# Spreading the gathering tokens' rows by three DRAM transfers in 4 KB runs, and turning 14 chunks of u early instead of 15

## The chip, the cores and the metric

The kernel runs on one core of a Trainium2 chip. Its time is the device time of one execution in microseconds (us). The engines are TensorE (PE in the profile, its weight loads PEld), VectorE (DVE), ScalarE (ACT), GpSimd (POOL) and SyncE (SP). Transfers are issued from the queues of SyncE, ScalarE and GpSimd, and run on 16 DMA engines that they share; the profile calls their packets q1 (SyncE's), q10 (ScalarE's) and q0 (GpSimd's).

## The reference

One decoder layer over 256 tokens of 1024 channels, in float32: a mixer (retention and block-sparse attention, merged by gates, with a residual), and then an expert layer, whose core is:

```python
def peer(h, w_q, sub_keys, u_tab, v_tab):       # h: 256 tokens x 1024
    q = (ht @ w_q).reshape(T, PEER_HEADS, 2, half)
    s = jnp.einsum('thcd,hcnd->thcn', q, sub_keys).astype(jnp.float32)
    s1, i1 = lax.top_k(s[:, :, 0], PEER_TOPK)
    s2, i2 = lax.top_k(s[:, :, 1], PEER_TOPK)
    ...
    top_s, pos = lax.top_k(cand_s, PEER_TOPK)
    experts = jnp.take_along_axis(cand_i, pos, axis=-1)
    gates = jax.nn.softmax(top_s, axis=-1).astype(h.dtype)
    ...
        u = u_tab[ec]
        a = jax.nn.gelu(jnp.einsum('td,thkd->thk', hc, u), approximate=False)
        return jnp.einsum('thk,thkd->td', gc * a, v_tab[ec])
```

There are 8 heads, 16 chosen experts each, and 16384 experts with a row of u and a row of v.

## The kernel before

The program has four stages. The mixer and the queries are a list of `pieces`: blocks of 256 x 512 of a weight matrix (512 KB), four to a unit of 512 output columns. A piece is loaded into one of six slots (`raw_ring`) by SyncE's queue (`load`, L191), split into a high part on ScalarE (L137, `rhi`) and a low part on VectorE (L138, `rlo`), and multiplied on TensorE in three products (L219 to L221, or L228 to L230). The main loops (L757 and L1001) go through the pieces in order: at step i they load piece i + 4 and beyond, split piece i + 3, multiply piece i, and then take one step (`pump`) of each of a few open tasks, generators that hold a unit's epilogue cut into parts. Each engine runs its instructions in the order in which they were written, so an instruction that waits holds up all that stands behind it on its engine; the DMA issues of ScalarE and GpSimd stand in their order too.

The query weights are the last 16 pieces (`peer_w_q`, four units). When a unit is complete, `queries` copies its result on ScalarE (L564), TensorE multiplies it with the sub-keys (L573), ScalarE scales the scores (L577), and VectorE chooses experts from them (`topk`). Two loads of sub-keys stand among the query pieces and hold two slots until TensorE has turned them (L788).

Then comes the u stage: all 16384 rows of u in 128 chunks of 128 rows. A chunk is loaded (L621), turned by eight TensorE transposes into `turn` (L666) with two evacuations on ScalarE (L667), and multiplied with the 144 dense tokens (L1137); meanwhile one-hot products build the dense gates (L1064). The other tokens gather only their chosen rows: 64 of them by one path, and 48 more (NX, three groups of 16, NXG x NXP) by a second. For the 48, the normed rows `h2x` are spread in DRAM so that each of the 8 heads has its own copy: `h2y`, shaped [3 groups, 8 heads, 16 tokens, 1024]. The u stage reads a group back as 128 rows in its first steps (`rows_x`, L1118, on ScalarE's queue). Last comes the v stage over 128 chunks of v.

The epilogue of the last mixer unit, `residual(1)`, does the spreading from GpSimd's queue, while the first query pieces are multiplied: h2x out to DRAM (L553), another row copy in SBUF (L554), then the spread (L556).

During the mixer, `early_turns` turns every eighth chunk of u ahead of time, NPRE of them, chunks 7, 15, 23 and so on: for each, four loads of 128 KB on ScalarE's queue (L677), two 32x32-block transposes on VectorE (L682) and a write of 512 KB to `turned` in DRAM (L679). In the u stage such a chunk is loaded from `turned` (L642), and TensorE skips its transposes. `early_turns` has two buffers in turn, named `eraw` and `h2` to read into, `eT` and `hTf` to write. The fifteenth, chunk 119, has its loads, transposes and write at steps 59 to 64 of the main loop, in the last units of the mixer.

Of the kernel before, what the change touches and what calls it, by code (L numbers as in the profile page):

```python
# [23 lines left out]
D = 1024  # L24
KC = D // P
H = 8
# [4 lines left out]
NXP = 16  # L31
NXG = 3
# [11 lines left out]
LAG_G = 2  # L44
SCRATCH = 88
TOPK = 16
NPRE = 15
STEP = 8
PRE0 = 20
WARM = 8  # L50
# [14 lines left out]
def layer_kernel(ctx, tc, x, mix_norm_g, w_in, ret_w_branch, moba_q_gain, moba_k_gain, moba_w_branch,  # L65
                 rel_bias, w_out, ffn_norm_g, peer_w_q, peer_sub_keys, peer_u, peer_v,
                 c_rope, c_decay, c_col, c_bucket, out, dbg=None):
    nc = tc.nc
# [18 lines left out]
    def side():  # L87
        return psum["side"].tile([P, 512], F32, name="side")
# [4 lines left out]
    def raw_tile(n=1):  # L93

        i = raw_count[0] % RAWS
        raw_count[0] += n
        assert i + n <= RAWS
        return raw_ring[:, i] if n == 1 else raw_ring[:, i:i + n]
# [36 lines left out]
    def split_to(hi, lo, src, engine=V):  # L135

        A.activation(hi, src, AF.Copy)  # L137
        engine.tensor_tensor(lo, src, hi.bitcast(F32), op=OP.subtract)  # L138
# [14 lines left out]
    h2x = dr.tile([NX, D], F32, name="h2x")  # L153
    h2y = dr.tile([NXG, H, NXP, D], F32, name="h2y")
# [5 lines left out]

    turned = dr.tile([NPRE, P, D], F32, name="turned")
    ident = cp.tile([P, P], F32, name="ident")
# [8 lines left out]
    def t4(shape, name, dt=F32):  # L171
        return wk.tile(shape, dt, name=name, tag="t4", bufs=3)

    def t2(shape, name):
        return wk.tile(shape, F32, name=name, tag="t2", bufs=4)
# [334 lines left out]
    def residual(j):  # L510
        def epi(o):

            xg = []
            for t in range(NT):
                c = slice(512 * j, 512 * (j + 1))
                V.tensor_tensor(xt[:, t, c], xt[:, t, c], o[t], op=OP.add)
            for t in range(NT):
                c = slice(512 * j, 512 * (j + 1))
                a = t2([P, 512], "xg")
                V.tensor_tensor(a, xt[:, t, c], grow2[:, c], op=OP.mult)  # L520
                sq = t2([P, 512], "sq2")
                A.activation(sq, xt[:, t, c], AF.Square, accum_out=ss2[:, j, t:t + 1])
                xg.append(a)
            yield
            yield
            for t in range(NT):
                p = side()
                for c in range(4):
                    T.transpose(p[:, c * P:(c + 1) * P], xg[t][:, c * P:(c + 1) * P], ident)
                split_to(qk_h[j][:, :, t * P:(t + 1) * P], qk_l[j][:, :, t * P:(t + 1) * P],  # L530
                         p.rearrange("p (c q) -> p c q", c=4))
            if j == 0:
                return
            nc.gpsimd.dma_start(x1d, xt)  # L534
            V.tensor_tensor(ss2[:, 0], ss2[:, 0], ss2[:, 1], op=OP.add)
            V.tensor_scalar(ss2[:, 0], ss2[:, 0], 1.0 / D, EPS, op0=OP.mult, op1=OP.add)
            G.tensor_tensor(r2, ss2[:, 0], minus_half[:, :NT], op=OP.pow)
            yield
            V.scalar_tensor_tensor(h2, xt[:, 0, :], r2[:, 0:1], grow2, op0=OP.mult, op1=OP.mult)
            hn = t4([P, D], "hn2")  # L540
            V.scalar_tensor_tensor(hn, xt[:, 1, :], r2[:, 1:2], grow2, op0=OP.mult, op1=OP.mult)
            yield
            for src, t0, n0, n in ((h2, NG, P, NA - P), (hn, 0, 0, P)):
                for q in range(2):
                    k = slice(4 * q, 4 * q + 4)
                    p = side()
                    for c in range(4):
                        T.transpose(p[:, c * P:(c + 1) * P], src.rearrange("p (i k) -> p k i", k=KC)[:, 4 * q + c], ident)
                    pv = p.rearrange("p (c q) -> p c q", c=4)[:, :, t0:t0 + n]
                    A.activation(hTf[:, k, n0:n0 + n], pv, AF.Copy)  # L550
                yield

            nc.gpsimd.dma_start(h2x, h2[P - NX:])  # L553
            nc.gpsimd.dma_start(h2[NG:], h2[:NG])  # L554
            yield
            nc.gpsimd.dma_start(h2y, h2x.rearrange("(n i) d -> n i d", n=NXG)[:, None].to_broadcast([NXG, H, NXP, D]))  # L556
            yield
        return epi

    def queries(q):  # L560
# [67 lines left out]
    def load_any(i):  # L628
# [9 lines left out]
        elif i < len(pieces) + NK:  # L638
            c = i - len(pieces)
            if c % STEP == STEP - 1 and c // STEP < NPRE:  # L640
                u_raw[c] = raw_tile()
# [14 lines left out]
    def transpose_u(c):  # L656

        if c < NK and c % STEP == STEP - 1 and c // STEP < NPRE:
            u_T[c] = u_raw.pop(c)
# [9 lines left out]
    def early_turns(i):  # L669

        m, step = divmod(i - PRE0, 3)
        if step == 0 and -1 <= m < NPRE - 1:

            c = STEP * (m + 1) + STEP - 1
            src = peer_u[0, c * P:(c + 1) * P, :].rearrange("(b a) (g d) -> g a b d", a=32, g=4)
            for g in range(4):
                nc.scalar.dma_start(early[0][(m + 1) % 2][32 * g:32 * g + 32].rearrange("a (b d) -> a b d", b=4), src[g])  # L677
        if step == 2 and 0 <= m < NPRE:
            nc.scalar.dma_start(turned[m], early[1][m % 2])  # L679
        if step < 2 and 0 <= m < NPRE:  # L680
            k = slice(4 * step, 4 * step + 4)
# [36 lines left out]
    for q in range(2):  # L718
        for t in range(NT):
            n = slice(t * P, (t + 1) * P)  # L720
            A.activation(hh[q][:, :, n], sides[2 * t + q], AF.Copy)
    for q in range(2):
        for t in range(NT):
            n = slice(t * P, (t + 1) * P)
# [397 lines left out]
    for c in range(NK):  # L1122
# [12 lines left out]
        for k in range(KC):  # L1135
            n = c % 2 * NA
# [142 lines left out]
```

## Time and profile before

| | us |
|---|---|
| median of three runs | 1034.11 |
| lowest and highest of them | 1033.67 to 1040.05 |
| the profiled execution, its own time | 1033.85 |
| its span, first to last instruction | 1031.8 |

The stages in that execution: mixer to about 256, queries to about 332, u stage to about 730, then the v stage. The page gives each engine's busy time, the span in 40 slices of 25.8 us, and the chain that ended last, followed back from the last instruction. In the rows of a timeline stand start, duration (of a merged group, from its first start to its last end), engine, line, operation, what is written and read, the shapes, and, in brackets, how long the engine had been idle and what ended it. Rows of a window hold its length and then each engine's busy time with the number of instructions; rows of a DMA queue hold packets, MB and the time that its packets took, as a share of 16 engines for the window's length. Two of the transfer rows of the page:

```profile
q0 software_dynamic: 27008, 96.82, 26.0%
...
raw_ring<-turned SPq DMA_DIRECT2D x15, 512.0 KB
```

### The profile page before, as it was taken

Reading aid. Unit: us, or ns where it says so; the run is one execution under the profiler, and the core shown is the slowest. Engines: PE = TensorE matmul, PEld = TensorE weight load, DVE = VectorE, ACT = ScalarE, POOL = GpSimd, SP = SyncE. Lnnn points to the kernel's source line nnn. Section 1 sums busy time; section 2 is a strip of 40 time slices with the busy share of each in tenths; the row PEclk is TensorE's granted clock in tenths of the full one; section 3 lists DMA queues with packets and bytes.
Section 4 is the critical chain, followed back from the end, with each engine's and each line's share of the span. In section 5 each row is a group of like instructions: output and inputs, shape, how many; then the busy total and the mean of one; then the engine's idle time right before and its main releaser. Section 6 shows DMA issues by size and latency. Waiting matters only on the chain.

```text
span 1031.8 us, 19502 instructions
## 1 busy us (share of the span) xinstructions
PE 1005.6 (97%) x7384; PEld 967.9 (94%) x7384; DVE 815.1 (79%) x1482; ACT 546.1 (53%) x991; POOL 307.0 (30%) x256
## 2 busy tenths in 40 slices
PE   8999999999949999999999999999999999999997
PEld 6887998997949999999999999999999999999997
DVE  6567667978548895699977999994788888888887
ACT  5545544534524434443346776679655555555553
POOL 2421000000102344444443443542433333333330
PEclk9999999999969999999999999999999999999999
DMA  9775787987735999899999787887799999999993
GB/s 332 194 201 169 235 247 212 301 269 225 239 123 162 383 372 352 330 367 373 376 384 344 280 284 255 285 320 244 270 345 345 352 336 345 348 343 345 341 347 108
DMA packets 103067, 301.43 MB, mean 292 GB/s; under 512 B 10740, under 2 KB 21005, under 8 KB 102822
## 3 DMA queue, kind: packets, MB, share of 16 engines
q1 hardware_dynamic: 64732, 186.07, 52.1%
q0 software_dynamic: 27008, 96.82, 26.0%
q10 hardware_dynamic: 11234, 17.31, 5.4%
q8 instruction: 58, 0.95, 0.4%
q14 instruction: 35, 0.29, 0.1%
HBM read 289.15 MB, written 12.00 MB: 292 GB/s over the span
## 4 chain that ended last, share of the span: by engine, by line
PE 89%; DMA 3%; DVE 3%; ACT 2%; issue 1%; ACTq 0%; POOL 0%; DVEq 0%; POOLq 0%
PE acc L1137 24%; PE acc L1170 19%; PE turn L666 10%; PE acc L1171 8%; PE gp L1064 4%; PE acc L228 3%; PE acc L229 3%; PE acc L230 3%; PE acc L219 3%; PE acc L220 3%; PE acc L221 3%; DMA raw_ring<-in_peer_w_q_dram 2%; PE side L573 1%; PE side L349 1%; PE side L374 1%
## 5 line engine op out<-in xcount | busy, mean ns | idle before, releaser
L924 POOL DMA_INDIRECT rows<-in_peer_u_dram,eg x112 | 140.0, 1250 | 130.0 <-DVE rows L935 50.4
L924 POOL DMA_INDIRECT rows<-in_peer_v_dram,eg x64 | 106.8, 1669 | 168.3 <-DVE vacc L998 167.4
L666 PE MATMUL turn<-ident,raw_ring 128*128 128x128 f32 x904 | 118.5, 274 | 0.8 <-ACT W L577 0.8
L666 PEld LDWEIGHTS turn<-ident,raw_ring 128*128 128x128 f32 x904 | 110.0, 191 | 1.0 <-ACT W L577 1.0
L935 DVE SCALAR_TENSOR_TENSOR rows<-rows,h 128x1024 f32<-128x1024 f32 x64 | 78.4, 1229 | 8.6 <-DMA rows<-in_peer_u_dram,eg 8.5
L998 DVE SCALAR_TENSOR_TENSOR vacc<-rows,av,vacc 128x1024 f32<-128x1024 f32 x63 | 80.6, 1279 | 0.0
L1108 ACT ACTIVATE cw<-W 128x384 fp32r<-128x384 f32 x64 | 33.7, 526 | 81.9 <-PE acc L1171 31.7
L1109 DVE TENSOR_TENSOR cw<-W,cw 128x384 fp32r<-128x384 f32 x64 | 36.3, 568 | 33.7 <-ACT cw L1108 33.7
L1079 ACT ACTIVATE W<-gp 128x512 f32<-128x512 f32 (+18 forms) x48 | 27.5, 577 | 41.4 <-DVE W L1077 35.0
L1030 ACT ACTIVATE oh_buf<-oh_buf,tT 128x128 f32<-128x128 f32 x128 | 40.9, 407 | 0.4 <-DVE oh_buf L1026 0.4
L1077 DVE TENSOR_TENSOR W<-gp,W 128x328 f32<-128x328 f32 (+17 forms) x36 | 36.5, 1015 | 5.3 <-PE gp L1064 5.0
L1094 POOL TENSOR_TENSOR W<-W,gl 128x288 f32<-128x288 f32 (+17 forms) x24 | 15.6, 651 | 83.9 <-ACT gl L1093 77.8
L935 DVE SCALAR_TENSOR_TENSOR rows<-rows,rlo__3191 128x1024 f32<-128x1024 f32 x16 | 19.4, 1217 | 21.1 <-DMA rows<-in_peer_u_dram,eg 21.0
L1064 PE MATMUL gp<-oh_buf 128*128 128x128 f32 x256 | 33.8, 276 | 0.0
L1137 PE MATMUL acc<-hTf,raw_ring 128*128 128x144 f32 x240 | 31.9, 286 | 0.0
L1064 PEld LDWEIGHTS gp<-oh_buf 128*128 128x128 f32 x256 | 31.5, 191 | 0.1
L1137 PEld LDWEIGHTS acc<-hTf,raw_ring 128*128 128x128 f32 x240 | 30.3, 190 | 0.0
L534 POOL DMA_DIRECT2D x1d<-xt x1 | 0.7, 652 | 91.7 <-DMA raw_ring<-in_peer_w_q_dram 91.7
L1025 DVE TENSOR_TENSOR oh_buf<-niota,tT 128x512 f32<-128x512 f32 x32 | 22.1, 690 | 7.0 <-PE gp L1064 6.4
L144 POOL TENSOR_TENSOR gny<-va,minus_half 128x8 f32<-128x8 f32 x2 | 3.3, 1653 | 79.1 <-DVE va L436 79.1
L935 DVE SCALAR_TENSOR_TENSOR rows<-rows,rlo__3252 128x1024 f32<-128x1024 f32 x16 | 19.3, 1218 | 9.4 <-DMA rows<-in_peer_u_dram,eg 9.4
L1026 DVE TENSOR_TENSOR oh_buf<-iota,tT 128x512 f32<-128x512 f32 x32 | 25.4, 793 | 0.0
(2091 smaller groups left out, 3491.2 us busy)
## 6 DMA issues: line engine op xcount, KB each, us to landing
raw_ring<-in_peer_v_dram SPq DMA_DIRECT2D x128, 512.0 KB
raw_ring<-in_peer_u_dram SPq DMA_DIRECT2D x113, 512.0 KB
raw_ring<-in_w_in_dram SPq DMA_DIRECT2D x52, 512.0 KB
raw_ring<-in_peer_w_q_dram SPq DMA_DIRECT2D x16, 512.0 KB
raw_ring<-turned SPq DMA_DIRECT2D x15, 512.0 KB
eraw<-in_peer_u_dram ACTq DMA_DIRECT2D x32, 128.0 KB
turned<-eT ACTq DMA_DIRECT2D x8, 512.0 KB
raw_ring<-in_ret_w_branch_dram SPq DMA_DIRECT2D x8, 512.0 KB
```

What stands on the lines that cost most here:

```text
L666: T.transpose(p[:, k * P:(k + 1) * P], r.rearrange("p (i k) -> p k i", k=KC)[:, 4 * q + k], ident)
L924: G.indirect_dma_start(out=r, out_offset=None, in_=tab, in_offset=bass.IndirectOffsetOnAxis(ap=eg[:, j:j + 1], axis=0))
L935: V.scalar_tensor_tensor(r, r, 1.0, h, op0=OP.mult, op1=OP.mult, accum_out=av[:, j:j + 1])
L998: V.scalar_tensor_tensor(gs["acc"], r, av[:, j:j + 1], gs["acc"], op0=OP.mult, op1=OP.add)
L1030: A.activation(o1[:, j], o1[:, j], AF.Copy, scale=tT[:, t, 2, k + j:k + j + 1])
L1064: T.matmul(p[:, j * P:(j + 1) * P], o2, o1, start=True, stop=True)
L1077: V.tensor_tensor(w[:, :, :c], p[:, :, :c], w[:, :, :c], op=OP.mult)
L1108: A.activation(w[:, :, :ND], W[:, c:c + 2, :], AF.Copy)
L1109: V.tensor_tensor(w[:, :, ND:], W[:, c:c + 2, :], w[:, :, :ND].bitcast(F32), op=OP.subtract)
L1137: T.matmul(pa[:, n:n + NA], uT[:, k * P:(k + 1) * P], hTf[:, k], start=(c % 2 == 0 and k == 0), stop=(k == KC - 1), skip_group_check=True)
L1170: T.matmul(o[b][:, :2 * ND], vh[:, n], w, start=(c == 0), stop=False, skip_group_check=True)
L1171: T.matmul(o[b][:, :ND], vl[:, n], w[:, :ND], start=False, stop=(c == NK - 1), skip_group_check=True)
```

## The change

```diff
-NPRE = 15
+NPRE = 14
...
             nc.gpsimd.dma_start(h2x, h2[P - NX:])
             nc.gpsimd.dma_start(h2[NG:], h2[:NG])
             yield
-            nc.gpsimd.dma_start(h2y, h2x.rearrange("(n i) d -> n i d", n=NXG)[:, None].to_broadcast([NXG, H, NXP, D]))
-            yield
+            for n in range(NXG):
+                src = h2x[NXP * n:NXP * (n + 1)]
+                nc.gpsimd.dma_start(h2y[n].rearrange("h i d -> i h d"), src[:, None, :].to_broadcast([NXP, H, D]))
+                yield
```

The spread of the 48 rows becomes three transfers, one for a group, with the 16 tokens outermost, the 8 copies inside them, and runs of one row (4 KB). Each is followed by a `yield`, so they go out in three steps of the task. And chunk 119 of u isn't turned early any more. Lines behind L556 move down by two in the changed kernel.

On GpSimd's queue, from the write of x1d to the first gathers of u; `h_74` is the tile of the normed rows. Before:

```order
L534 DMA x1d<-xt 128x2048
L537 TENSOR_TENSOR r_75<-ss_116,minus_half 128x2
L553 DMA h2x<-h_74 48x1024
L554 DMA h_74<-h_74 64x1024
L556 DMA h2y<-h2x 24x1x16384
L867 DMA eg<-ei 64x16
L924 DMA rows<-in_peer_u_dram,eg 128x1024 x5
```

After:

```order
L534 DMA x1d<-xt 128x2048
L537 TENSOR_TENSOR r_75<-ss_116,minus_half 128x2
L553 DMA h2x<-h_74 48x1024
L554 DMA h_74<-h_74 64x1024
L558 DMA h2y<-h2x 16x8x1024 x3
L869 DMA eg<-ei 64x16
L926 DMA rows<-in_peer_u_dram,eg 128x1024 x5
```

One transfer of 24 blocks of 16 rows became three of 16 x 8 single rows, in the same place.

On VectorE, near the end of the mixer, where chunk 119 was turned (`sa` and `ml` belong to the epilogue of a mixer unit, `rlo` are low parts of weights). Before:

```order
L138 TENSOR_TENSOR rlo__2196<-raw_ring,rhi__2195 128x1024
L682 STREAM_TRANSPOSE eT<-eraw 128x4x4x32
L138 TENSOR_TENSOR rlo__2226<-raw_ring,rhi__2225 128x1024
L504 TENSOR_TENSOR sa<-sa,acc 128x512
L505 TENSOR_TENSOR sa<-sa,sb 128x512
L138 TENSOR_TENSOR ml_139<-sa,mh_137 128x512
L504 TENSOR_TENSOR sa<-sa,acc 128x512
L505 TENSOR_TENSOR sa<-sa,sb 128x512
L138 TENSOR_TENSOR ml_139<-sa,mh_137 128x512
L682 STREAM_TRANSPOSE eT<-eraw 128x4x4x32
L138 TENSOR_TENSOR rlo__2264<-raw_ring,rhi__2263 128x1024
```

After (the numbers of the tiles shift a little):

```order
L138 TENSOR_TENSOR rlo__2192<-raw_ring,rhi__2191 128x1024
L138 TENSOR_TENSOR rlo__2221<-raw_ring,rhi__2220 128x1024
L504 TENSOR_TENSOR sa<-sa,acc 128x512
L505 TENSOR_TENSOR sa<-sa,sb 128x512
L138 TENSOR_TENSOR ml_139<-sa,mh_137 128x512
L504 TENSOR_TENSOR sa<-sa,acc 128x512
L505 TENSOR_TENSOR sa<-sa,sb 128x512
L138 TENSOR_TENSOR ml_139<-sa,mh_137 128x512
L138 TENSOR_TENSOR rlo__2258<-raw_ring,rhi__2257 128x1024
```

The two transposes are gone and nothing else moved; ScalarE's queue loses the four loads and the write.

On TensorE, in the u stage at chunk 119. Before:

```order
L1064 MATMUL gp<-oh_buf 128x128 x4
L1137 MATMUL acc<-hTf,rhi__6986 128x144 x8
L1064 MATMUL gp<-oh_more 128x128 x4
L666 MATMUL turn<-ident,raw_ring 128x128 x8
L1137 MATMUL acc<-hTf,rhi__7023 128x144 x8
L1064 MATMUL gp<-oh_buf 128x128 x4
L666 MATMUL turn<-ident,raw_ring 128x128 x8
L1137 MATMUL acc<-hTf,raw_ring 128x144 x8
```

After:

```order
L1066 MATMUL gp<-oh_buf 128x128 x4
L668 MATMUL turn<-ident,raw_ring 128x128 x8
L1139 MATMUL acc<-hTf,rhi__6981 128x144 x8
L1066 MATMUL gp<-oh_more 128x128 x4
L668 MATMUL turn<-ident,raw_ring 128x128 x8
L1139 MATMUL acc<-hTf,rhi__7018 128x144 x8
L1066 MATMUL gp<-oh_buf 128x128 x4
L668 MATMUL turn<-ident,raw_ring 128x128 x8
L1139 MATMUL acc<-hTf,rhi__7059 128x144 x8
```

Chunk 119 gets the eight transposes that every untouched chunk has (and two evacuations on ScalarE), and its products read the turned copy in place of the loaded rows.

## The prediction

> **What bounds the kernel now.** I read the page first: busy time per engine, the slices, the chain that ended last.
>
> ```profile
> span 1031.8 us, 19502 instructions
> PE 1005.6 (97%) x7384; PEld 967.9 (94%) x7384; DVE 815.1 (79%) x1482; ACT 546.1 (53%) x991; POOL 307.0 (30%) x256
> PEclk9999999999969999999999999999999999999999
> PE 89%; DMA 3%; DVE 3%; ACT 2%; issue 1%; ACTq 0%; POOL 0%; DVEq 0%; POOLq 0%
> ```
>
> TensorE bounds the program: busy for 97% of the span, and 89% of the chain. So an edit is worth what it puts on or takes off TensorE's time, and the only places with something to take off are those where TensorE stands. The twelfth slice of the clock, a 6 among nines, is one. The windows around it, and the chain of waits in order of time there, say what it is:
>
> ```profile
> 270.00:280.00 10.00, 10.00 (x88) 10.00 (x88) 3.33 (x5) 5.92 (x10) 0.37 (x1) 1.00 0.72 218
> 280.00:290.00 10.00, 5.62 (x47) 5.42 (x46) 2.17 (x16) 0.59 (x1) 0.00 (x0) 0.89 0.41 163
> 290.00:300.00 10.00, 1.32 (x6) 1.32 (x7) 3.16 (x15) 3.09 (x4) 0.00 (x0) 0.50 0.36 121
> 300.00:310.00 10.00, 10.00 (x68) 10.00 (x68) 8.49 (x37) 4.17 (x5) 0.00 (x0) 0.76 0.46 155
> ...
> 275.24 21.74 DMA raw_ring<-in_peer_w_q_dram
> ```
>
> In the windows the columns are TensorE, its weight loads, VectorE, ScalarE, GpSimd, then the granted clock, the DMA share and GB/s. TensorE is full until 285, nearly empty to 298, and then runs at a clock of 0.50, mean 0.76 in the ten us after. What ended last was a load of a query-weight piece that took 21.74 us, with DMA only 0.36 to 0.46 busy: it was blocked, not short of bandwidth. The timelines of GpSimd, SyncE's queue and ScalarE:
>
> ```profile
> 269.74 0.63 POOL L556 DMA_DIRECT2D h2y<-h2x  x1
> ...
> 271.50 0.37 SPq L191 DMA_DIRECT2D raw_ring<-in_peer_w_q_dram  x1
> 275.24 0.37 SPq L191 DMA_DIRECT2D raw_ring<-in_peer_w_q_dram  x1
> ...
> 279.90 0.69 ACT L577 ACTIVATE W<-side,r 128x512 f32<-128x512 f32 x1 [0.21 <-PE side L573]
> 295.75 1.06 ACT L137 ACTIVATE rhi__2735<-raw_ring 128x1024 fp32r<-128x1024 f32 x1 [15.16 <-DMA raw_ring<-in_peer_w_q_dram]
> ...
> 298.68 3.78 PE L573 MATMUL side<-skT,W 128*128 128x128 f32 x16 [13.06 <-ACT W L564]
> ```
>
> The load of 271.50 (of the piece that rhi__2735 splits) was issued just behind h2y, the transfer that the change rewrites. ScalarE stood 15.16 us for it, the copy L564 was queued behind, and TensorE stood 13.06 us for that copy. The DMA queues from 284.1 to 292, the middle of the stall (packets, MB, share of 16 engines):
>
> ```profile
> q0 software_dynamic: 9, 0.59, 17.5%
> ...
> q1 hardware_dynamic: 9, 0.02, 0.6%
> ```
>
> q0 (GpSimd's queue) moves nine packets of 0.59 MB / 9 = 65 KB, each 0.175 x 16 x 7.9 / 9 = 2.46 us, on 0.175 x 16 = 2.8 engines at a time: h2y, 24 packets for three engines, 8 x 2.46 = 20 us. q1 (the weights) gets nine of 2 KB in the same time: one behind each big one. Every weight piece is spread over all the engines and waits for its last packets on those three.
>
> **The change, part by part.** (1) The three transfers. Each spreads 16 rows, eight times over: 128 packets of 4 KB, 384 in all instead of 24, same 1.5 MB. GpSimd issues two more transfers at about 0.63 us each; between 270.4 and the next thing that it does it has nothing to do:
>
> ```profile
> 321.11 0.55 POOL L867 DMA_DIRECT2D eg<-ei  x1 [50.74 <-DVE i12f L876]
> ...
> 334.19 0.33 ACTq L1118 DMA_DIRECT2D rlo__3191<-h2y  x1
> ```
>
> so they cost nothing on the path, and the rows are read back only at 334. What a 4 KB packet from DRAM to DRAM takes, the trace doesn't show. From below: a sixteenth of the 65 KB packet, 0.154 us. From above: the 4 KB packets from SBUF to SBUF (L554), alone on the engines in the window 270.2 to 271.4:
>
> ```profile
> q0 software_dynamic: 59, 0.24, 90.8%
> ```
>
> 0.908 x 16 x 1.2 / 59 = 0.30 us, on 14.5 engines at once. I take 0.2, nearer to the lower end, because the old packets are the only ones that go from DRAM to DRAM. With 24 packets for each of 16 engines that is 4.8 us (3.7 to 7.2). A weight piece is 256 packets of 2 KB, 16 an engine, whose price is in the window 276 to 282:
>
> ```profile
> q1 hardware_dynamic: 793, 1.54, 76.4%
> ```
>
> 0.764 x 16 x 6 / 793 = 0.092 us, 1.5 us a piece. Worst case, all of h2y goes first: the loads of 271.50 and 275.24 are through 3.0 + (3.7 to 7.2) = 6.7 to 10.2 us after about 272.5 (the first issue, and a us that I allow for the start), at 279 to 283. These are times of before; part (2) moves all of them alike. The first is wanted when ScalarE is free at 280.6, and shares the engines with h2y packet by packet: 16 x (0.092 + 0.2) = 4.7 us, there at 277. The second has to be split (1.06 us) ahead of L564, which TensorE allows at 285.3, so it is wanted by 284.2. Both make it, at both ends of the bound. The stall then goes as a whole; how much that is, I read by laying the same place of the next unit, which has no stall, beside it:
>
> ```profile
> 285.34 0.28 PE L230 MATMUL acc<-hh,rlo__2640 128*128 128x256 f32 x1
> 302.12 0.56 PE L228 MATMUL acc<-hh,rhi__2682 128*128 128x256 f32 x1
> 304.81 0.29 PE L228 MATMUL acc<-hh,rhi__2682 128*128 128x256 f32 x1
> ...
> 314.77 0.28 PE L230 MATMUL acc<-hh,rlo__2831 128*128 128x256 f32 x1
> 317.15 0.36 PE L228 MATMUL acc<-hh,rhi__2877 128*128 128x256 f32 x1
> 318.66 0.28 PE L228 MATMUL acc<-hh,rhi__2877 128*128 128x256 f32 x1
> ```
>
> From the last product of a unit to the thirteenth of the next (L573's 16 small products lie between): 318.66 - 314.77 = 3.89 us without the stall, 304.81 - 285.34 = 19.47 with it, by when the clock is full again. The difference, 15.58 us, is the stall and its cold clock (13.06 and 2.52).
>
> Why three engines, and will it be sixteen? The trace shows both kinds: 2.8 engines for h2y, 14.5 for the 64 rows of L554. In the Trainium skill, "DMA: Bandwidth & Descriptors", section "Queues, rings and completion order", the number of engines is the largest up to 16 that divides the slowest dimension of both sides. That gives 3 for h2y now (3 groups against 24 blocks), which agrees with the 2.8 above, and 16 after the change (16 rows on both sides); without that rule the sum goes by the row of L554.
>
> (2) The fifteenth early chunk leaves the mixer: four loads that ScalarE's queue issues, two transposes on VectorE, a write of 512 KB. VectorE there, two rows of the chain of waits, ScalarE and TensorE:
>
> ```profile
> 231.08 1.22 DVE L682 STREAM_TRANSPOSE eT<-eraw 128x512 f32<-128x512 f32 x1
> 238.75 1.17 DVE L682 STREAM_TRANSPOSE eT<-eraw 128x512 f32<-128x512 f32 x1
> 239.84 1.18 DVE L138 TENSOR_TENSOR rlo__2264<-raw_ring,rhi__2263 128x1024 fp32r<-128x1024 f32 x1
> ...
> 232.30 1.11 DVE rlo__2226 L138
> ...
> 237.48 0.64 ACT mh L137
> ...
> 238.01 1.04 ACT L137 ACTIVATE rhi__2263<-raw_ring 128x1024 fp32r<-128x1024 f32 x1
> ...
> 241.08 0.50 PE L220 MATMUL acc<-rlo__2264,mh 128*128 128x512 f32 x1 [1.46 <-DVE rlo__2264 L138]
> ```
>
> TensorE stands 1.46 us for rlo__2264. The chain runs from the first transpose through VectorE and ScalarE to ScalarE's mh, right ahead of rhi__2263, so without that transpose all of this comes 1.2 us earlier. Without the second, rlo__2264 starts when rhi__2263 is there, at 239.05 - 1.2 = 237.85 instead of 239.84, and ends at 239.0, before TensorE asks for it at 239.6. All of the 1.46 us goes. With the second alone it would be 0.8 (239.05 for 239.84): my lower end. The freed issues and the write lie on queues that nobody waits for once this is gone.
>
> (3) The same chunk, 119, is turned by TensorE in the expert stage instead. The chain has the price, where any chunk stands:
>
> ```profile
> 336.95 0.89 PE turn L666 x8
> 337.84 1.96 PE acc L1137 x16
> ...
> 660.00:670.00 10.00, 10.00 (x87) 10.00 (x87) 10.00 (x13) 5.72 (x20) 6.07 (x6) 1.00 0.54 161
> ```
>
> +0.89 us of TensorE, all of it on the path, since TensorE has no gap in that stage. Two evacuations on ScalarE (2 x 0.54 us) fit: it is 5.72 of 10 us busy there. VectorE is full, but gets no more work, only 0.89 us more time. The load is the same 512 KB from another place.
>
> Sum: 1033.85 (this execution's own time; 2 us lie around its span) - 15.58 - 1.46 + 0.89 = 1017.7 us. Its own time is 0.26 us under the median of the runs shown, so I give it unchanged.
>
> **The rivals.** A shorter stall stays: 4 KB packets now stand on every engine, not on three. It begins when 3.0 + 24 x p passes 284.2 - 272.5 = 11.7 us, at p = 0.36 us a packet, above my bound of 0.30; at 0.5 us the stall is 3.3 us, and the time 1021. A gap of 1.46 us left the clock full:
>
> ```profile
> 240.00:250.00 10.00, 8.68 (x40) 6.85 (x41) 8.96 (x11) 7.16 (x11) 0.00 (x0) 1.00 0.77 255
> ```
>
> one of 13.06 did not, so up to 1.3 us of cold clock may be added, for 1022 to 1023. The Trainium skill ("TensorE: Matmul & The Clock Gate", Part 1) has the clock recover after about 3.4 us of sustained work. By it today's cold clock would be worth 1.7 us; the rows above have it last from 298.68 to 304.8 and cost 2.52, and they decide. Chance 0.13.
>
> The change doesn't do what it says: the transfers stay on few engines. Then 384 packets x 0.2 / 3 = 26 us, but each weight packet there waits for a 4 KB packet, not for one of 65 KB: 16 x 0.29 = 4.7 us a piece, 9.4 for the first two, there at 282. Even that stalls little: about 1018 to 1022, as the later pieces come every 4.7 us to a TensorE that wants one about every 3.3. 0.07.
>
> VectorE takes over, with the top-k work no longer hidden by the stall. From where the stall ends to where the last query piece is split:
>
> ```profile
> 296.84:320.33 23.49, 19.62 (x59) 0.83 0.45 147
> ```
>
> 19.62 us of VectorE's work for that. Begun at 281.7 it ends at 301.4 at the earliest; TensorE comes to that piece at about 310 (the eighth from 285.34 + 2.38 = 287.7: seven of 24 x 0.12 = 2.9 us, and 2.3 for the next L573). It has 8 us in hand; chance 0.03, time up to 1021.
>
> Slower than before: the same mechanism as the first rival, with a packet so dear that all sixteen engines block longer than three do. Stall and cold clock are back to today's when 3.0 + 24 x p reaches 11.7 + 13.06, at p = 0.91 us; 1% slower, 1044, needs about 1.4 us. Against it: three times the upper end of the bound. 0.03.
>
> **How the numbers follow.** My forecast, 1017.7, has 0.74; with the ends of its terms (0.8 for 1.46; L573's copy or a load late by a us or so) it is 1016.5 to 1020. The range takes in the shorter stall: 1016 to 1023. About 1% is what a measurement of this kernel can tell from no change, here 1023.8 and 1044.5. Faster: the forecast, VectorE, nearly all of the shorter stall and of the few engines, 0.91. Same: the rest of these, 0.06. Slower 0.03.
>
> **What would show it.** Right: no idle time of TensorE above 2 us between 230 and 320, PEclk 9 in all slices, the chain without DMA on the query weights; 384 q0 packets of 4 KB within some 8 us after the issue; TensorE without a gap at L220; one more group of eight transposes. Wrong: ScalarE waiting for a query piece around 280, which by its length gives the packet's price, or a new wait of TensorE for VectorE behind it.

## The result, and the profile after

| | before | changed |
|---|---|---|
| median of four runs | 1034.72 us | 1017.54 us |
| lowest and highest | 1033.67 to 1040.05 | 1016.8 to 1020.45 |
| the profiled execution, its own time | 1033.85 | 1016.8 |
| its span | 1031.8 | 1015.0 |

The ratio is 0.9839, with a 95% interval of 0.9814 to 0.9864: the kernel is 1.4 to 1.9% faster. The forecast was 1017.7 us.

The page of the changed kernel, busy time of each engine, the clock in 40 slices, and the shares of the chain that ended last:

```profile
span 1015.0 us, 19518 instructions
...
PE 1003.3 (99%) x7392; PEld 966.3 (95%) x7392; DVE 812.3 (80%) x1480; ACT 547.3 (54%) x993; POOL 303.2 (30%) x258
...
PEclk9999999999999999999999999999999999999999
...
PE 95%; ACT 2%; DVE 1%; DMA 1%; issue 1%; ACTq 0%; POOL 0%; SPq 0%; DVEq 0%; POOLq 0%
```

TensorE's busy time is about what it was (1003.3 us for 1005.6); the span around it is 16.8 us shorter. The 6 among the nines is gone, and the chain has 1% DMA left of 3%. The windows that were half empty before, columns as there:

```profile
270.00:280.00 10.00, 10.00 (x87) 10.00 (x87) 4.70 (x18) 5.47 (x8) 0.00 (x0) 1.00 0.99 321
280.00:290.00 10.00, 9.97 (x82) 9.57 (x81) 8.39 (x44) 5.82 (x8) 0.00 (x0) 1.00 0.72 252
290.00:300.00 10.00, 9.97 (x82) 9.57 (x81) 9.86 (x16) 4.10 (x6) 0.00 (x0) 1.00 0.52 165
...
230.00:320.00 90.00, 89.12 (x652) 83.69 (x652) 71.58 (x188) 44.65 (x67) 9.74 (x13) 1.00 0.70 224
```

TensorE works through all of them, at a granted clock of 1.00 (before: 5.62 and 1.32 us of ten, clock 0.89 and 0.50). From 230 to 320 it is idle for 0.88 us in all. What stands in the place of the 13 us stall, first ScalarE (the splits of two query pieces, then the copy L566, which was L564), then TensorE:

```profile
279.12 1.06 ACT L137 ACTIVATE rhi__2730<-raw_ring 128x1024 fp32r<-128x1024 f32 x1 [0.50 <-DMA raw_ring<-in_peer_w_q_dram]
280.69 1.06 ACT L137 ACTIVATE rhi__2769<-raw_ring 128x1024 fp32r<-128x1024 f32 x1 [0.51 <-DMA raw_ring<-in_peer_w_q_dram]
283.03 1.31 ACT L566 ACTIVATE W<-acc 128x512 f32<-128x512 f32 x2 [1.28 <-PE acc L230]
...
283.37 0.28 PE L230 MATMUL acc<-hh,rlo__2635 128*128 128x256 f32 x1
283.68 2.32 PE L575 MATMUL side<-skT,W 128*128 128x128 f32 x16
285.75 0.37 PE L228 MATMUL acc<-hh,rhi__2677 128*128 128x256 f32 x1
```

ScalarE still waits for both loads, by half a us each instead of 15.16 us for one. It then waits 1.28 us for TensorE at L566: the loads came 1.28 us before they would have held anyone up.

To see where the time went I compare when TensorE starts the same instruction in both kernels, which needs no reading of idle time:

| place | this step | after minus before, so far |
|---|---|---|
| start of the mixer's main part (differs from run to run) | +0.45 | +0.45 |
| the products around L220, near 240 | -1.79 | -1.34 |
| the products around L529, near 246, and little bits up to the queries | -0.63 | -1.97 |
| from the last product of the second query unit to the thirteenth of the third | -15.57 | -17.54 |
| chunk 119 in the u stage | +0.89 | -16.65 |
| end of the v stage | -0.04 | -16.69 |

The steps give 16.7 of the 16.8 us by which the spans differ.

### The profile page after: what moved, and what is told of

It is laid out like the page before. It is cut to its first block, busy times and chain, and to the rows that moved or that the text cites. A ratio compares the mean times of both kernels' runs of the same rounds, so it can differ in the third digit from the quotient of the medians.

```text
span 1015.0 us, 19518 instructions
## 1 busy us (share of the span) xinstructions
PE 1003.3 (99%) x7392; PEld 966.3 (95%) x7392; DVE 812.3 (80%) x1480; ACT 547.3 (54%) x993; POOL 303.2 (30%) x258
## 4 chain that ended last, share of the span: by engine, by line
PE 95%; ACT 2%; DVE 1%; DMA 1%; issue 1%; ACTq 0%; POOL 0%; SPq 0%; DVEq 0%; POOLq 0%
PE acc L1139 25%; PE acc L1172 19%; PE turn L668 10%; PE acc L1173 9%; PE acc L228 4%; PE acc L229 4%; PE acc L230 4%; PE gp L1066 4%; PE acc L219 4%; PE acc L220 3%; PE acc L221 3%; PE side L575 1%; PE side L349 1%; DMA raw_ring<-in_w_in_dram 1%; PE side L374 1%
## 5 line engine op out<-in xcount | busy, mean ns | idle before, releaser
L926 POOL DMA_INDIRECT rows<-in_peer_u_dram,eg x112 | 136.5, 1218 | 133.7 <-DVE rows L937 52.3
L1139 PE MATMUL acc<-hTf,raw_ring 128*128 128x144 f32 x224 | 29.8, 286 | 0.0
```

Source lines behind the costliest of these rows:

```text
L926: G.indirect_dma_start(out=r, out_offset=None, in_=tab, in_offset=bass.IndirectOffsetOnAxis(ap=eg[:, j:j + 1], axis=0))
L1139: T.matmul(pa[:, n:n + NA], uT[:, k * P:(k + 1) * P], hTf[:, k], start=(c % 2 == 0 and k == 0), stop=(k == KC - 1), skip_group_check=True)
```

## The experiments

My theory: the stall came from packets of 65 KB on three engines, behind which each weight packet there stood in turn; the time h2y holds its fullest engine, and the size of its packets, set how late the weights come. Rivals: that the early chunk alone frees the queues; that the new form helps only because it is spread over 16 engines; that the weights simply go last whatever the packets are. Unless it says otherwise, an edit is made to the changed kernel.

**The two parts apart.** The new transfers with 15 early chunks:

```diff
-NPRE = 14
+NPRE = 15
```

> The three transfers without the other part (15 early chunks again). Theory (the stall is h2y's 65 KB packets on three engines, and nothing else): TensorE's stall of 13 us at the third query unit is gone, the mixer's stall at L220 is back, and the u stage has one group of eight transposes less: 1016.8 + 2.4 - 0.9 = 1018.3 us. Rival (the early chunk's loads and write, ending some 30 us ahead of it, have a share in the stall): some of the stall stays, 1021 to 1030 us.

Measured: 1019.37 us, ratio 0.9855 (0.9839 to 0.9871). The step of the stall is -15.58 us again, and TensorE's gap at L220 is back, to the hundredth:

```profile
242.24 0.50 PE L220 MATMUL acc<-rlo__2264,mh 128*128 128x512 f32 x1 [1.46 <-DVE rlo__2264 L138]
```

Its profiled execution (1020.5) also lost about a us each at two gaps that differ from run to run: the start (+1.15 where the changed kernel had +0.45), and a wait in the u stage for ScalarE near 540. So the medians' difference of 1.8 us agrees with parts (2) and (3), 2.41 - 0.89 = 1.52 us by the changed kernel's trace, only roughly; the trace is the better witness.

The other half: the old transfer with 14 early chunks:

```diff
-            for n in range(NXG):
-                src = h2x[NXP * n:NXP * (n + 1)]
-                nc.gpsimd.dma_start(h2y[n].rearrange("h i d -> i h d"), src[:, None, :].to_broadcast([NXP, H, D]))
-                yield
+            nc.gpsimd.dma_start(h2y, h2x.rearrange("(n i) d -> n i d", n=NXG)[:, None].to_broadcast([NXG, H, NXP, D]))
+            yield
```

> 14 early chunks with the old single transfer. Theory: the 13 us stall stays with its cold clock, shifted as a whole by what the mixer gains (1.8 us at L220 and 0.6 us at L529, start to start), and 0.9 us of transposes come in the u stage: 1033.85 - 2.4 + 0.9 = 1032.3 us. Rival (what the mixer gains is lost again in the stall, because its end is set by transfers and not by TensorE): 1033.9 + 0.9 = 1034.8 us.

Measured: 1031.53 us, ratio 0.9975 (0.9966 to 0.9985). ScalarE and TensorE in the stall:

```profile
293.65 1.06 ACT L137 ACTIVATE rhi__2728<-raw_ring 128x1024 fp32r<-128x1024 f32 x1 [15.01 <-DMA raw_ring<-in_peer_w_q_dram]
...
296.66 1.65 PE L573 MATMUL side<-skT,W 128*128 128x128 f32 x6 [12.99 <-ACT W L564]
```

The stall is there as before (12.99 for 13.06 us), some 2 us earlier, so the early chunk didn't cause it. But the cold clock behind it is shorter. TensorE working at a clock of 0.50, in the kernel before and then here:

```profile
298.68:304.70 6.02, 6.02 (x28) 6.02 (x29) 4.58 (x27) 2.76 (x4) 0.00 (x0) 0.50 0.59 201
296.66:299.70 3.04, 3.04 (x14) 3.04 (x15) 3.00 (x15) 1.12 (x2) 0.00 (x0) 0.50 0.63 213
```

Start to start, stall and cold clock together cost 1.4 us less than before, which the expectation didn't have: a stall of the same length doesn't always leave the same stretch of slow clock. The transfers bring nearly everything; the chunk alone brings 2.6 us by the medians (1034.1 to 1031.53). Start to start it gives 2.41 us in the mixer and takes 0.89 in the u stage; the shorter cold clock makes about the rest.

**Same big packets, more engines.** One transfer with the 8 heads outermost, so that packets of 65 KB go to eight engines, three each:

```diff
-            for n in range(NXG):
-                src = h2x[NXP * n:NXP * (n + 1)]
-                nc.gpsimd.dma_start(h2y[n].rearrange("h i d -> i h d"), src[:, None, :].to_broadcast([NXP, H, D]))
-                yield
+            nc.gpsimd.dma_start(h2y.rearrange("n h i d -> h n (i d)"),
+                                h2x.rearrange("(n i) d -> n (i d)", n=NXG)[None].to_broadcast([H, NXG, NXP * D]))
+            yield
```

> The spread as one transfer with the heads outermost: the same 24 blocks of 64 KB, so the same packets of 65 KB, but 8 engines of 3 packets in place of 3 engines of 8. Theory (what counts is how long the fullest engine is taken, here 3 x 2.46 = 7.4 us against 20): the first query load lands about a us later than with the 4 KB runs, the stall is 0 to 2 us, 1016.8 to 1019 us. Rival (a weight packet behind each packet of 65 KB is what hurts, on any number of engines): eight engines hold up every piece, the stall stays at 8 us or more, 1025 to 1034 us.

Measured: 1018.16 us, ratio 0.9851 (0.9834 to 0.9867), as the changed kernel. ScalarE and TensorE at the place of the stall:

```profile
281.42 1.06 ACT L137 ACTIVATE rhi__2728<-raw_ring 128x1024 fp32r<-128x1024 f32 x1 [2.23 <-DMA raw_ring<-in_peer_w_q_dram]
...
284.42 2.14 PE L574 MATMUL side<-skT,W 128*128 128x128 f32 x16 [0.21 <-ACT W L565]
```

GpSimd's DMA queue from 270 to 278, while the spread runs:

```profile
q0 software_dynamic: 71, 1.52, 49.3%
```

That is 0.493 x 16 = 7.9 engines. ScalarE waits 2.23 us for the first piece, TensorE 0.21. So 4 KB runs aren't needed: big packets do next to no harm where an engine has only three of them. By the old price that is 3 x 2.46 = 7.4 us; the 24 packets ran from 269.9 to 279.1, 9.2 us, and were through just as ScalarE began to want the first piece.

**Three engines, smaller packets.** Here the transfer at this place is a copy of rows of u that nobody reads, as many bytes as the spread, on three engines; the real spread, unchanged, goes out in the expert choice of the first unit instead, on the same queue behind the first gather's indices. With runs of 4080 bytes:

```diff
+    spare = dr.tile([NXG, P + 2, D], F32, name="spare")
...
-            for n in range(NXG):
-                src = h2x[NXP * n:NXP * (n + 1)]
-                nc.gpsimd.dma_start(h2y[n].rearrange("h i d -> i h d"), src[:, None, :].to_broadcast([NXP, H, D]))
-                yield
+            src = peer_u[0, :NXG * (P + 2)].rearrange("(n r) d -> n r d", n=NXG)
+            nc.gpsimd.dma_start(spare[:, :P, :D - 4], src[:, :P, :D - 4])
+            yield
...
+            for n in range(NXG if q == 0 else 0):
+                src = h2x[NXP * n:NXP * (n + 1)]
+                nc.gpsimd.dma_start(h2y[n].rearrange("h i d -> i h d"), src[:, None, :].to_broadcast([NXP, H, D]))
```

> In the place of the spread stands a copy of rows of u in 3 x 128 runs of 4 KB that nobody reads (three outermost, so three engines, 128 packets each, 1.5 MB); the real spread follows in its three transfers behind the first small transfer of expert indices, some 33 us later. It asks which of the two mattered, packet size or engine count. By packet size (a weight packet waits for one packet ahead of it, now 0.2 us): a piece takes 16 x 0.29 = 4.7 us on those engines, the stall is 0 to 3 us, 1017 to 1021 us. By engine count (what was issued first on an engine goes first, whatever its packets; with the 4 KB runs no weight packet moved for 3.8 us after the issue): three engines are taken for 128 x 0.16 to 0.2 = 20 to 26 us, and the stall of 10 to 16 us is back: 1028 to 1035 us.

Measured: 1025.18 us, ratio 0.9915 (0.9898 to 0.9931), between the two. The size wasn't what I had asked for: the copy ran as packets of 8 KB (192 of 8160 bytes, beside 832 of 8 bytes). The DMA queues of its profile from 288 to 292, in the stall (packets, MB, share of 16 engines):

```profile
q0 software_dynamic: 32, 0.26, 15.4%
...
q1 hardware_dynamic: 44, 0.07, 4.7%
```

A packet takes 0.154 x 16 x 4 / 32 = 0.31 us, and the weights get 44 for 32 of them. TensorE there:

```profile
291.26 2.08 PE L575 MATMUL side<-skT,W 128*128 128x128 f32 x8 [6.77 <-ACT W L566]
```

The stall is 6.77 us: half of 13, with the same 20 us of packets (64 x 0.31) on each of three engines. Neither expectation held: 1025.18 lies between 1017 to 1021 and 1028 to 1035. Start to start this place costs 8.1 us more than in the changed kernel, stall and cold clock together, of the 8.8 us by which the spans differ; so the spread's later place costs little.

With runs of 2 KB, which came out as 384 packets of 4 KB beside 1664 of 8 bytes:

```diff
-            src = peer_u[0, :NXG * (P + 2)].rearrange("(n r) d -> n r d", n=NXG)
-            nc.gpsimd.dma_start(spare[:, :P, :D - 4], src[:, :P, :D - 4])
+            src = peer_u[0, :NXG * (2 * P + 2)].rearrange("(n r) d -> n r d", n=NXG)
+            nc.gpsimd.dma_start(spare[:, :2 * P, :D // 2], src[:, :2 * P, :D // 2])
```

> As the kernel that put a copy on three engines, which came out with packets of 8 KB and a stall of 6.8 us; now in 3 x 256 runs of 2 KB, the same 1.5 MB on three engines, with packets of at most 4 KB. Theory (on an engine that both use, weights and copy go one packet for one, so a piece takes 16 x (packet + 0.09) us there; 65 KB gave 13 us of stall, 8 KB 6.8): with 4 KB packets at 0.16 us a piece takes 4 us, two take 8, the second is there at about 281, stall 0 to 1 us, 1017 to 1019 us; with 2 KB packets none. Rival (a long queue on three engines costs several us whatever the packets): stall 5 to 7 us as with 8 KB, 1023 to 1026 us.

Measured: 1022.52 us, ratio 0.9873 (0.9848 to 0.9898). The DMA queues of its profile from 290 to 292:

```profile
q0 software_dynamic: 26, 0.11, 12.9%
...
q1 hardware_dynamic: 29, 0.06, 7.1%
```

One for one again, at 0.129 x 16 x 2 / 26 = 0.16 us a packet. TensorE at the place of the stall and one unit on:

```profile
286.28 0.97 PE L575 MATMUL side<-skT,W 128*128 128x128 f32 x6 [1.66 <-ACT W L566]
...
303.31 1.91 PE L575 MATMUL side<-skT,W 128*128 128x128 f32 x9 [3.44 <-ACT W L566]
```

The time missed the 1017 to 1019 us of the theory. Its price of a piece held, 4 us, and the first stall is small (1.66 us for 0 to 1). I had left out that the copy goes on to 300: every later piece is slowed too, comes each 3.9 us to a TensorE that wants one per 3.5 (a unit of four takes 13.87 us in the changed kernel), and TensorE stands 3.44 us at the next unit. Just behind that gap the clock falls to 0.50, and both together make the place 4.8 us longer start to start:

```profile
303.85:307.20 3.35, 3.35 (x18) 3.35 (x17) 2.21 (x3) 1.13 (x2) 0.00 (x0) 0.50 0.60 204
```

This profiled execution (1024.37 us) is the slowest of four, which reach down to 1019.42, so the second stall need not be as long in each. On three engines the stalls thus go 13.06, 6.77, and 1.66 with 3.44, for packets of 65, 8 and 4 KB. Both things count: the packet's size, as a weight packet waits out one of them each time, and how long the fullest engine is held. One difference stays open: the copies' packets of 8 bytes, which the spread doesn't have.

**The spread done twice.** Each of the three transfers goes out a second time, into a copy that nobody reads, so that all 16 engines have 48 packets each:

```diff
+    h2z = dr.tile([NXG, H, NXP, D], F32, name="h2z")
...
                 nc.gpsimd.dma_start(h2y[n].rearrange("h i d -> i h d"), src[:, None, :].to_broadcast([NXP, H, D]))
+                nc.gpsimd.dma_start(h2z[n].rearrange("h i d -> i h d"), src[:, None, :].to_broadcast([NXP, H, D]))
```

> The changed kernel with every spread transfer done twice, the second copy to a place that nobody reads: 48 packets of 4 KB for each engine in place of 24. It measures how much room is left before TensorE stands again. In the changed kernel no weight packet moved until most of the spread was through, the two query loads in question landed at 279.1 and 280.7, and the second split ended 1.3 us ahead of its need. Theory A (the spread goes first as a whole): 24 x 0.16 = 3.9 us more, loads at 283 and 284.7, TensorE stands about 3 us, 1019.5 to 1021.5 us. Theory B (weights and spread share the engines packet by packet, as the prediction had it): the first piece is at most 16 x 0.16 us later than alone, no stall, 1016.8 to 1018 us.

Measured: 1019.32 us, ratio 0.9857 (0.9835 to 0.9879). TensorE's wait:

```profile
286.75 2.09 PE L577 MATMUL side<-skT,W 128*128 128x128 f32 x16 [3.15 <-ACT W L568]
```

The window around it, columns as before:

```profile
280.00:290.00 10.00, 6.85 (x59) 6.64 (x57) 6.04 (x31) 4.89 (x7) 0.00 (x0) 1.00 0.98 358
```

And the DMA queues from 274 to 280:

```profile
q0 software_dynamic: 365, 1.34, 58.2%
...
q1 hardware_dynamic: 356, 0.70, 42.5%
```

The stall is as theory A had it, about 3 us (the time lies 0.2 us under its range), and the clock stays at 1.00 over it. Its picture, that the whole spread goes ahead of the weights, isn't what the queues show: 365 packets of the spread to 356 of the weights is one for one. What matters for the changed kernel is that the single spread had 1.28 us in hand, and one twice as long has none.

**How many early chunks, and where.** Thirteen; then fifteen and sixteen with the first begun earlier (PRE0, the step of the main loop at which the early turning starts), so that the last is done before VectorE gets short:

```diff
-NPRE = 14
+NPRE = 13
```

> The changed kernel with 13 early chunks. Theory (an early chunk is worth 0.88 us of TensorE's time in the u stage, and costs only where its two transposes make TensorE stand in the mixer, which the fourteenth doesn't): 1016.8 + 0.9 = 1017.7 us. Rival (each early chunk costs the mixer as the fifteenth did): 1016.8 + 0.9 - 2.4 = 1015.3 us.

```diff
-NPRE = 14
+NPRE = 15
...
-PRE0 = 20
+PRE0 = 17
```

> 15 early chunks, begun three steps of the main loop sooner (PRE0 17 in place of 20), so that the last pair of transposes stands where the fourteenth's stood, with the three transfers. Theory (the place of the fifteenth costs, not their number): no stall at L220, one group of transposes less, 1016.8 - 0.9 = 1015.9 us. Rival (the loads of early chunks meet the mixer's weights at its start, where a TensorE gap opens): 1017 to 1019 us.

```diff
-NPRE = 14
+NPRE = 16
...
-PRE0 = 20
+PRE0 = 14
```

> 16 early chunks, begun six steps sooner (PRE0 14): the same once more. Theory: 1016.8 - 1.8 = 1015.0 us. Rival: the mixer's start gets a gap of over a us, 1016 to 1019 us.

Measured, all three beside the same runs of before: 1018.52 us (0.985, 0.9827 to 0.9873), 1016.24 (0.9832, 0.9807 to 0.9857) and 1016.1 (0.9831, 0.9808 to 0.9853). The medians are in the expected order, the first and the last 0.8 and 1.1 us above what was expected and the second 0.3 above, but their intervals overlap each other's and that of the changed kernel, so the runs alone don't rank them. The traces do. With fifteen from step 17, TensorE passes L220 without a wait, and ends 17.15 us ahead of before:

```profile
240.22 0.39 PE L220 MATMUL acc<-rlo__2265,mh 128*128 128x512 f32 x1
```

With sixteen it gains another 0.89 us in the u stage, to -17.86 at the end. In the one with thirteen, the u stage takes 2.67 us more than before, where two chunks make 1.77; a gap near 537, of the kind that differs between runs, makes the rest. The mixer's main part starts 0.83 us later than before with fifteen and 1.10 with sixteen (0.45 in the changed kernel); runs whose early chunks begin at step 20 spread from 0.41 to 1.43, so this doesn't tell whether the earlier loads cost anything there. An early chunk is therefore worth its 0.89 us as long as its transposes don't fall where TensorE waits for VectorE, and the stall at L220 was a matter of where the fifteenth stood, not that there were fifteen.

## Why the prediction was right

**The stall.** Predicted 15.58 us with its cold clock, from two rows of one place laid beside two of the next; measured 15.57, and 15.58 with the transfers alone. The cold clock's part, 2.52 us, is what this execution of the kernel before had: with the old transfer and fourteen chunks a stall of the same length came to 14.15 us in all. That the cause was h2y's packets on few engines is shown from both sides: take the engines' load down with the packets left big (eight engines), and the stall goes; leave three engines and make the packets smaller, and it shrinks with them.

**Where its working was off.** I took 0.2 us for a 4 KB packet from DRAM to DRAM, between 0.154 and 0.30. The DMA queues of the changed kernel, first while the spread runs (269.6 to 273.2), then up to when the second load lands (273.2 to 280.6):

```profile
q0 software_dynamic: 350, 1.30, 96.7%
...
q1 hardware_dynamic: 1012, 1.96, 87.1%
q0 software_dynamic: 79, 0.25, 10.4%
```

SyncE's queue, where the loads are issued:

```profile
269.53 4.63 SPq L191 DMA_DIRECT2D raw_ring<-in_peer_w_q_dram  x3
```

0.967 x 16 x 3.6 / 350 = 0.16 us: the lower end, as the old packet's sixteenth said. But the first load was said to share the engines with the spread "packet by packet, there at 277" in times of before. It didn't: it was issued at 269.53, and no packet of the weights moved until 273.2, when most of the spread was through (0.25 of its 1.5 MB were left). After that 1012 packets of weights went by, about four pieces, until the second of the two wanted pieces was in: loads behind it shared the engines with it. The price of a packet was a little too high; the time until a load starts (a us allowed, 3.7 measured) and the other loads beside it were taken too low. What I called the worst case was "at 279 to 283", 277 to 281 in this kernel, whose queries begin 2 us earlier; the two loads came at 279.1 and 280.7, in its upper half. The forecast stood because the bound, and not the sharing, carried the conclusion. That bound was nearer to its limit than I wrote: the spread done twice shows what was behind it. The spread's packets came within 8.4 us of the first issue, some 8 being the sign given, but for two that ended later, the last at 277.8.

**The early chunk.** This term was mis-sized: 1.46 us, measured 1.79 + 0.62 = 2.41. The mechanism was right, VectorE's two transposes ahead of rlo__2264; the mistake was in taking the idle time of the row for the loss. TensorE's rows of before, at the two places, and then the same two in the changed kernel:

```profile
239.16 0.45 PE L219 MATMUL acc<-rhi__2263,mh 128*128 128x512 f32 x1
241.42 0.40 PE L221 MATMUL acc<-rhi__2263,ml 128*128 128x512 f32 x1
...
246.24 0.39 PE L221 MATMUL acc<-rhi__2283,ml 128*128 128x512 f32 x1
246.87 0.93 PE L529 MATMUL side<-ident,xg 128*128 128x128 f32 x5 [0.24 <-DVE xg L520]
247.88 0.48 PE L219 MATMUL acc<-rhi__2300,mh 128*128 128x512 f32 x1
```

```profile
239.62 0.39 PE L219 MATMUL acc<-rhi__2257,mh 128*128 128x512 f32 x1
240.08 0.40 PE L221 MATMUL acc<-rhi__2257,ml 128*128 128x512 f32 x1
...
244.90 0.39 PE L221 MATMUL acc<-rhi__2276,ml 128*128 128x512 f32 x1
245.92 0.47 PE L219 MATMUL acc<-rhi__2293,mh 128*128 128x512 f32 x1
```

From L219 to L221 it is 2.26 us before and 0.46 after; from L221 to the next L219 1.64 and 1.02. Undisturbed, a product starts every 0.23 us and is shown as 0.39 us long, since matmuls overlap. So idle time that is counted from a shown end is too short: the product at L220 could have started at 239.39, and the 1.46 us count from 239.61; the next one then came 0.34 us behind it, not 0.23. Together 1.46 + 0.22 + 0.11 = 1.79. In the same way 0.24 stands for 0.62. This second wait for VectorE I had passed over altogether. It hangs on the same transposes: with the transfers alone both waits are there, and with fifteen chunks begun at step 17 both are gone, again 2.41 us start to start.

**Chunk 119.** Predicted +0.89 us, measured +0.89, TensorE having no gap there. The chunk before, and then in the changed kernel with its new group of transposes:

```profile
688.54 1.05 PE L1064 MATMUL gp<-oh_buf 128*128 128x128 f32 x8
689.43 2.13 PE L1137 MATMUL acc<-hTf,rhi__6986 128*128 128x144 f32 x16
...
671.01 1.05 PE L1066 MATMUL gp<-oh_buf 128*128 128x128 f32 x8
671.90 1.05 PE L668 MATMUL turn<-ident,raw_ring 128*128 128x128 f32 x8
672.78 2.13 PE L1139 MATMUL acc<-hTf,rhi__6981 128*128 128x144 f32 x16
```

From the start of the one-hot products to that of the chunk's own it is 0.89 us before and 1.77 after.

**The sum and its luck.** By the profiled executions the terms make -15.57 - 2.41 + 0.89 = -17.09, and the mixer's start, which differs from run to run, gave +0.45 back: -16.64 of the span's -16.8, for a forecast of -16.15. A miss of 0.95 us in one term was half covered by that jitter. The forecast also started from an execution 0.87 us under the median of before's four runs: from median to median the kernel gained 17.18 us. That 1017.7 came within 0.2 us of the median of 1017.54 is luck; that it came within about a us isn't.

**The rivals.** A shorter stall didn't come (packets at 0.16 us, not 0.36). The transfers did go to all engines (96.7% of 16 while the spread ran). The rule on the number of engines, which in the Trainium skill's "DMA: Bandwidth & Descriptors" stands in the section "Why a DMA increments its semaphore by 16 and not by 1", agrees with the three forms of the spread: 2.8 engines measured for three, 7.9 for eight, 15.5 for sixteen. VectorE didn't take over: it is 9.86 of 10 us busy from 290 to 300, with TensorE at 9.97 beside it. What the rival of few engines said, that 4 KB packets on three engines would come out at 1018 to 1022 through the later pieces, is what the run with 4 KB packets on three engines gave, 1022.52, half a us above it. Nor did the kernel get slower.

## What to carry to other kernels

A transfer that nobody is in a hurry for can still cost time, when it shares DMA engines with loads that are wanted: look at how many engines it holds, for how long the fullest, and how big its packets are, since a small packet behind it waits out one big one each time. Spreading it over more engines took the stall away here, with small packets on sixteen and with big ones on eight. And to price a stall, lay starts beside starts at a place of the same code without it; the idle time that a row shows leaves out the overlap of matmuls and the cold clock.

## What I hadn't expected of the hardware

With the spread on all 16 engines the weights' first packet came 3.7 us after its load's issue (269.53 to 273.2), and much the same with the spread done twice, though the latter had as much again still to move; from then on the queues took turns. With the big packets on eight engines it came 2.3 us after the issue, and where the transfer was on three 1.3 to 1.7 us. Why a transfer on more engines delays the start, no run here shows. Nor did I expect runs of 4080 and of 2048 bytes to come out as packets of 8 KB and 4 KB: a run's length in the code isn't the packet's, which has to be read from the trace. And TensorE's clock: 3.15 us without work left it at 1.00 (the spread done twice), 3.44 us were followed by a slow stretch (the 4 KB copy on three engines), and so were 6.77 and 13 us. Once work was back after the two stalls of 13 us, the clock stayed at 0.50 for 3.0 us in one kernel and for 6 in the other.
